# Expert weights of a mixture-of-experts stage in tiles of 256 whole rows instead of 512 half rows

## Chip, cores and metric

The kernel runs on one core of a Trainium2 chip. The metric is the device time of one execution, in microseconds (us); less is better.

## What is computed

The program is one mixing layer, a mixture-of-experts stage and two further layers on 512 tokens of 1024 channels. Only the middle stage is touched. Cut to what matters:

```
affinity = softmax(h @ w_router)                      # 512 tokens, 16 experts
gate_vals, tok_idx = top_k(affinity^T, 64)            # each expert takes 64 tokens
xs  = h[tok_idx]                                      # [16, 64, 1024]
hid = silu(xs @ w_gate[e]) * (xs @ w_up[e])           # per expert, 1024 x 1024 each
ye  = (hid @ w_down[e]) * gate_vals
out = zeros(512, 1024).at[tok_idx].add(ye)
```

The three weight matrices of an expert are 1024 x 1024 in float32, 4 MB each: 16 experts x 3 x 4 MB = 201 MB, each byte of which is read once.

## The kernel before

All names are of `_body`. Phase B (lines 1340 to 1673) is the experts' stage. It takes the 16 experts in eight pairs (`for p in range(8)`, L1585). A pair's 128 slots stand in the 128 partitions, 64 for each expert.

**The weights.** The list `wseq` (L1359 to L1364) says in which order tiles come. A tile is 1 MB: 512 rows of the matrix by half of its columns, [128, 4, 512] in SBUF, so each row of a tile is 2 KB contiguous in DRAM (`src`, L1379). A pair has 24 tiles, the program 192. `wload` (L1369) issues the next tile on SP's queue (L1381; the last two tiles in halves, L1387). The tiles rotate through `NW` = 11 buffers, and the 12th and 13th tile go into `macc`, which is still empty then. 13 tiles are issued ahead of the first use (L1391); afterwards `experts` calls `wload` twice each time it has used two tiles, and SP waits until the buffer's last reader has finished.

**The products.** `experts(p, W, n, lhs)` (L1539) fills one PSUM bank `pe` with 512 output columns (half `n`) for both experts, from four tiles: for each of 8 row blocks one matmul for each expert, in 64 of the array's columns each (L1551). One such matmul is recorded as two instructions.

**A pair, in the program's order.** For each half `n`: gate, then up (each four tiles), silu on ACT (L1618), the product with up on DVE (L1619), four transposes on PE (L1622) and a copy into `hidT` (L1623). In half 0 the slots' gates `gcol` and the transposed one-hot `ohT` are made besides (L1604 to L1616). Then `gather(p + 1)` (L1556) fetches the next pair's tokens by one-hot products (L1563, L1564) and transposes them into `xg` (L1570). Then, for each half of the output columns: down (four tiles), the scaled result split into `yh` on ACT (L1632) and `yl` on DVE (L1633), and the scatter: for four blocks of tokens two products with `ohT` (L1637, L1638), added into `macc` by DVE (L1643).

**PSUM.** Four banks with tag "g" for `pe`, four with tag "p" for all else (L1536). **The order.** A scheduler in the framework fixes the order on each engine when the program is built, which need not be the program's own; each engine then runs its list in sequence and waits only for data and buffers.

After the last pair the sums become the residual `xres` (L1651 to L1667), and phase C starts with the transposes at L1695.

```
            if i < len(wseq) - 2:
                nc.sync.dma_start(t, src)
...
                for e in range(2):
                    PE.matmul(o[64 * e:64 * e + 64], lhs(k, e), w[e][:, kk], start=k == 0, stop=k == 7)
            wload()
            wload()
```

Of the kernel before, what the change touches and what calls it, by code (L numbers as in the profile page):

```python
# [10 lines left out]
F32 = mybir.dt.float32  # L11
# [10 lines left out]
D = 1024  # L22
RH = 8
C = 64
# [103 lines left out]
def _body(tc, nc, st, A, out, dbg, stop):  # L128
# [13 lines left out]
    def rsqrt(pool, v, n, add, mul=1.0):  # L142
        """1/sqrt(v*mul+add) of a small tile v[:, :n], by Newton's steps."""
# [22 lines left out]
    # ---------------------------------------------------------------- phase A  # L166
# [52 lines left out]
    # silu(c) for the modulation: t = tanh(c/2); (t+1)*c = 2*silu(c)  # L219
# [30 lines left out]
    def mod_vec(j):  # L250
        """shift (j = 0, 1) or scale (2, 3) of 512 channels, by channel"""
# [11 lines left out]
    # normalised tokens, channel-major, split into two float32r parts  # L263
# [26 lines left out]
    def context():  # L290
        """what the first products need last: the context, and the other half of the channels"""
# [23 lines left out]
    def tok_major(c0, blocks, first=False):  # L315
        """blocks of h @ w_in[:, c0:c0+512], token-major, in PSUM"""
# [62 lines left out]
    def take():  # L379
        """the feed's next weights; the next but one are loaded and the next split before their products"""  # L380
# [7 lines left out]
    def ch_major(c0, ctxt, w=None):  # L388
        """(h @ w_in[:, c0:c0+128]).T in PSUM: the 512 tokens, and the context's 256"""
# [11 lines left out]
    # ------------------------------------------------------------ retention  # L401
# [7 lines left out]
    def late(t, name):  # L409
        """a table that is loaded no sooner than the modulation is there"""  # L410
# [15 lines left out]
    def rope_tok(dst, src, b, i):  # L426
        """rotary embedding of 8 heads, token-major (i = 1: times 1/8)"""
# [7 lines left out]
    def to_ch(dst, src, b):  # L435
        """dst[:, pair, b*128:...] = src.T for the four pairs of heads; dst: tiles and their partitions"""
# [8 lines left out]
    # each pair's heads, the other one's channels zero  # L445
# [83 lines left out]
    # gates, head norm: silu(g) * y * rsqrt(mean(y^2) + eps); t = tanh(g/2); (t+1)*g = 2*silu(g)  # L529
# [3 lines left out]
    def head_bcast(rs, pr, i, n):  # L533
        """rs: two parts of a row for each head of the pairs; every channel's of a pair"""
# [6 lines left out]
    # sums of squares over a head's 64 rows, in row 32*pair + 2*direction + head  # L541
# [37 lines left out]
    # ----------------------------------------------------------------- rwkv  # L579
# [5 lines left out]
    def wide(name, tag="W3", bufs=3):  # L585
        """one block of 128 channels: the 512 tokens, then the context's 256"""
# [20 lines left out]
    # 0 where a chunk begins, 1 elsewhere  # L607
# [23 lines left out]
    def mod_rest():  # L631
        """partial sums of the rest of the modulation's columns, for later; a step for every 256 rows"""
# [54 lines left out]
    # the retention's half of mix @ w_out  # L687
# [25 lines left out]
    # iclr = sigmoid(a0 + al @ a2) from th = tanh(z/2); kk = k*k_k / max(|k*k_k|, 1e-12)  # L713
# [13 lines left out]
    # sigmoid of the gates' inner columns  # L727
# [8 lines left out]
    # gt1*g_post_mix, g_pre_ffn*(1+sc2), sh2, gt2*g_post_ffn in rows 0, 32, 64, 96  # L736
# [34 lines left out]
    for pr in range(4):  # L771
# [28 lines left out]
        # cumulated decays of both directions, and what they multiply; direction 1 has a chunk's tokens reversed  # L800
# [24 lines left out]
        # the gates, and these times lnx_w  # L825
# [12 lines left out]
        # bonus + lnx_b, times the sum of the gates  # L838
# [66 lines left out]
    def batch(members, act):  # L905
        """four units (block of tokens, direction): products of their chunks' b, k with a, r"""
# [74 lines left out]
        # T21^T = T11^T A21^T T22^T  # L981
# [39 lines left out]
    def ready(u):  # L1021
        """what the chain needs of a unit: token-major b, k and v, decayed a and r above their products"""
# [26 lines left out]
    def decayed(u):  # L1049
        """a and r in place of b's products with them, which have been used"""  # L1050
# [8 lines left out]
    def step(u, c, ci, last):  # L1059
        """one chunk: u.UV[:, c] holds (state, v), then (u, v)"""  # L1060
# [55 lines left out]
    def spare(i):  # L1116
        """2 KB pieces of what held the context's products"""
# [6 lines left out]
    def finish(units):  # L1124
        """head norm of both units' outputs; gates and bonus, channel-major"""
# [54 lines left out]
    def chain(pair, last):  # L1180
        """two chunks of both directions, half a step apart"""
# [10 lines left out]
    class Weave:  # L1192
        """generators of work that is traced between others', at given rates"""
# [23 lines left out]
    def run(pairs, last=False):  # L1217
        """the chain over some pairs of units, directions alternating; the next pair is made ready meanwhile"""
# [63 lines left out]
    def load_out():  # L1282
        """the other half of w_out, in two parts; gt1*g_post_mix; g_pre_ffn*(1+sc2) and sh2 by channel"""
# [33 lines left out]
    # ---- mix @ w_out: the rwkv's half, in blocks of tokens as they end  # L1317
# [22 lines left out]
    # -------------------------------------------------- phase B: experts  # L1340
# [11 lines left out]
    # the mix and x; in their places the normed tokens' two parts  # L1352
# [16 lines left out]
    def wload():  # L1369
        i = wnext[0]  # L1370
        if i < len(wseq):
            W_, e, half, n = wseq[i]
            if NW <= i < NW + 2:
                # the sum of the experts is empty yet
                t = macc[:, 2 * (i - NW):2 * (i - NW) + 2].rearrange("p b (h n) -> p (b h) n", h=2)
# [27 lines left out]
    def rsqrt1(v):  # L1403
        """1/sqrt(v/D + EPS) of a column: the square root's reciprocal and one of Newton's steps"""
# [9 lines left out]
    # the router's weights times the gain, and its products with the shift  # L1414
# [9 lines left out]
    def mixed(tb):  # L1424
        """x + gt1 * rms_norm(mix)"""
# [873 lines left out]
```

## Time and profile before

| | us |
|---|---|
| median of 3 runs (2916.70 to 2926.42) | 2918.49 |
| span of the profiled execution | 2929.8 |
| own time of the profiled execution | not given beside its span |
| experts' products, first to last | 818.6 to 1316.9 |
| PE busy over the span | 2724.7 (93%) |

The profile is of one execution; times in it count from the span's start. PE is the matmul engine, PEld its weight load, DVE, ACT, POOL the vector, scalar and general engines, SP the engine that issues most DMAs. A view by stretches gives each engine's busy time in that stretch, the granted PE clock as a share of full speed, the mean busy share of the 16 DMA engines (it can read over 1, since a packet's time runs from read to write) and the rate at which they moved bytes.

### The profile page before, as it was taken

To read this page: it belongs to the slowest core of one execution; us is meant where nothing else is said; L and a number is where in the kernel's file an instruction comes from. 1 tells how busy PE (TensorE), PEld (TensorE's weight loads), DVE (VectorE), ACT (ScalarE), POOL (GpSimd) and SP (SyncE) were. 2 spreads that over 40 slices of the span, in tenths; PEclk is the share of its full clock that TensorE was granted. 3 is DMA by queue.
4 is the path that set the end of the run, shared out by engine and by line. 5 is a ranking of instruction groups with operands and counts; after the bars stand their busy time and mean duration, and the time that the engine had idled before them with its cause. 6 is when DMAs were issued, how large, how long until landed. Compare 5 with 4: busy or idle time off the path is not lost.

```text
span 2929.8 us, 38119 instructions
## 1 busy us (share of the span) xinstructions
PE 2724.7 (93%) x15198; PEld 1930.5 (66%) x15198; DVE 1358.2 (46%) x2452; ACT 1026.0 (35%) x1988; POOL 266.3 (9%) x266
## 2 busy tenths in 40 slices
PE   7999997578899888888999999989999999999999
PEld 5767555457743333336778767867888888888887
DVE  4354286897611111116545655456334444444333
ACT  4232353356421101115445534643223332333223
POOL 1102044545100000002000000000000000000000
PEclk9999977789899999998999989988999999999999
DMA  6305755546779999993212311232222333223332
GB/s 244 87 15 175 233 163 160 140 113 167 265 291 386 386 387 387 387 373 116 58 58 72 102 51 51 65 117 64 94 94 94 94 91 96 88 93 94 94 94 93
DMA packets 300433, 456.33 MB, mean 156 GB/s; under 512 B 32367, under 2 KB 127160, under 8 KB 299744
## 3 DMA queue, kind: packets, MB, share of 16 engines
q1 hardware_dynamic: 283376, 438.44, 45.0%
q10 hardware_dynamic: 13632, 7.79, 0.9%
q0 software_dynamic: 3248, 7.67, 0.8%
q8 instruction: 120, 1.97, 0.3%
q14 instruction: 57, 0.47, 0.0%
HBM read 425.45 MB, written 28.40 MB: 155 GB/s over the span
## 4 chain that ended last, share of the span: by engine, by line
PE 67%; DMA 7%; DVE 6%; ACT 1%; issue 1%; POOL 0%; SPq 0%; DVEq 0%; ACTq 0%; POOLq 0%
PE acc L1771 10%; PE acc L1773 10%; PE acc L1772 10%; PE pe L1551 8%; PE accb L162 6%; PE accb L163 6%; PE accb L164 6%; DMA wexp<-in_w_up 3%; DMA wexp<-in_w_gate 2%; PE pS L2053 2%; DVE zT L971 1%; DVE zZ L973 1%; PE po L2105 1%; PE pt L1936 1%; DMA xres<-sx 1%
## 5 line engine op out<-in xcount | busy, mean ns | idle before, releaser
L159 DVE TENSOR_TENSOR wlo<-wc,whi 128x1024 fp32r<-128x1024 f32 x238 | 291.2, 1224 | 483.3 <-ACT whi L158 468.8
L158 ACT CAST whi<-wc 128x1024 fp32r<-128x1024 f32 x240 | 251.8, 1049 | 499.6 <-PE acc L1772 313.9
L1771 PE MATMUL acc<-whi,yHi 128*128 128x512 f32 x640 | 274.1, 430 | 5.0 <-DVE xres L1805 4.6
L163 PE MATMUL accb<-y2Lo,whi 128*128 128x512 f32 x704 | 278.4, 395 | 0.0
L162 PE MATMUL accb<-y2Hi,whi 128*128 128x512 f32 x704 | 277.6, 396 | 0.1
L164 PE MATMUL accb<-y2Hi,wlo 128*128 128x512 f32 x704 | 277.5, 395 | 0.0
L1551 PE MATMUL pe<-wexp,xg 128*64 128x512 f32 x1008 | 245.0, 597 | 30.7 <-DMA wexp<-in_w_up 21.3
L1773 PE MATMUL acc<-wlo,yHi 128*128 128x512 f32 x640 | 257.5, 403 | 0.0
L1772 PE MATMUL acc<-whi,yLo 128*128 128x512 f32 x640 | 256.5, 401 | 0.0
L1771 PE MATMUL acc<-whi,aHi 128*128 128x512 f32 x512 | 202.7, 396 | 0.0
L1772 PE MATMUL acc<-whi,aLo 128*128 128x512 f32 x512 | 202.6, 396 | 0.0
L1773 PE MATMUL acc<-wlo,aHi 128*128 128x512 f32 x512 | 202.5, 396 | 0.0
L1551 PEld LDWEIGHTS pe<-wexp,xg 128*64 128x64 f32 x1008 | 77.0, 136 | 174.8 <-issue 122.5
L1771 PEld LDWEIGHTS acc<-whi,yHi 128*128 128x128 f32 x640 | 130.9, 205 | 42.4 <-issue 15.4
L162 PEld LDWEIGHTS accb<-y2Hi,whi 128*128 128x128 f32 x704 | 131.9, 187 | 32.7 <-ACT whi L158 0.5
L163 PEld LDWEIGHTS accb<-y2Lo,whi 128*128 128x128 f32 x704 | 132.0, 187 | 32.4 <-DVE y2Lo L1698 0.3
L164 PEld LDWEIGHTS accb<-y2Hi,wlo 128*128 128x128 f32 x704 | 132.0, 187 | 32.1
L1773 PEld LDWEIGHTS acc<-wlo,yHi 128*128 128x128 f32 x640 | 130.6, 204 | 28.5 <-issue 4.6
L1772 PEld LDWEIGHTS acc<-whi,yLo 128*128 128x128 f32 x640 | 131.5, 205 | 20.4 <-issue 1.4
L1551 PE MATMUL pe<-wexp,hidT 128*64 128x512 f32 x512 | 123.8, 597 | 1.9 <-DMA wexp<-in_w_down 1.9
L1771 PEld LDWEIGHTS acc<-whi,aHi 128*128 128x128 f32 x512 | 96.2, 188 | 23.2
L1773 PEld LDWEIGHTS acc<-wlo,aHi 128*128 128x128 f32 x512 | 96.2, 188 | 23.2
(654 smaller groups left out, 4617.9 us busy)
## 6 DMA issues: line engine op xcount, KB each, us to landing
wc<-in_mlp_w SPq DMA_DIRECT2D x128, 512.0 KB
wexp<-in_w_gate SPq DMA_DIRECT2D x63, 1024.0 KB
wexp<-in_w_up SPq DMA_DIRECT2D x63, 1024.0 KB
wexp<-in_w_down SPq DMA_DIRECT2D x62, 1024.0 KB
wc<-in_a_wqkv SPq DMA_DIRECT2D x72, 512.0 KB
wmod<-in_w_mod SPq DMA_DIRECT2D x32, 512.0 KB
w_b<-in_w_in SPq DMA_DIRECT2D x24, 512.0 KB
wc<-in_b_win SPq DMA_DIRECT2D x24, 512.0 KB
```

Source lines behind the costliest of these rows:

```text
L158: ACT.copy(hi, src)
L159: eng.tensor_tensor(lo, src, hi.bitcast(F32), op=OP.subtract)
L162: PE.matmul(o, whi, xhi, start=first, stop=False)
L163: PE.matmul(o, whi, xlo, start=False, stop=False)
L164: PE.matmul(o, wlo, xhi, start=False, stop=last)
L971: V.tensor_tensor(tm, Z[:, j + 1:, j:j + 1].to_broadcast([128, m, j]), Z[:, j:j + 1, :j].to_broadcast([128, m, j]), op=OP.mult)
L973: V.tensor_tensor(Z[:, j + 1:, :j], Z[:, j + 1:, :j], tm, op=OP.add)
L1551: PE.matmul(o[64 * e:64 * e + 64], lhs(k, e), w[e][:, kk], start=k == 0, stop=k == 7)
L1771: PE.matmul(acc[b], xh, hi[:, kk], start=k == 2 * halves[0], stop=False)
L1772: PE.matmul(acc[b], xl, hi[:, kk], start=False, stop=False)
L1773: PE.matmul(acc[b], xh, lo[:, kk], start=False, stop=k == 2 * halves[-1] + 1)
L2053: PE.matmul(pS[:, x * wd + lo:x * wd + hi], qT[r, pr, b * 128:(b + 1) * 128], kT[r, pr, ks], start=True, stop=True)
```

## The change

Each tile holds 256 whole rows of a matrix, [128, 2, 1024], 4 KB contiguous in DRAM, still 1 MB. `expert_quarter` uses two such tiles (one for each expert) for both halves of the output columns, so gate, up and down each accumulate in two PSUM banks at once. Silu for both halves follows gate, the product with up for both halves follows up. `gather` and `scatter` become generators: the scatter's split into `yh` and `yl` follows down, its products are kept in `owed` and run after the first two quarters of the next pair's gate. The last pair's down keeps the old tiles and order (`expert_half`, which is the old `experts`, and an immediate scatter). Buffers, their number and the number of loads stay. Lines that only lose a comment are left out here; they shift line numbers.

```diff
-        for n, W_ in ((0, "w_gate"), (0, "w_up"), (1, "w_gate"), (1, "w_up"), (0, "w_down"), (1, "w_down")):
-            for half in range(2):
-                for e in range(2):
-                    wseq.append((W_, 2 * p_ + e, half, n))
+        for W_ in ("w_gate", "w_up"):
+            wseq += [(W_, 2 * p_ + e, i, None) for i in range(4) for e in range(2)]
+        if p_ < 7:
+            wseq += [("w_down", 2 * p_ + e, i, None) for i in range(4) for e in range(2)]
+        else:
+            wseq += [("w_down", 2 * p_ + e, half, n) for n in range(2) for half in range(2) for e in range(2)]
...
-                t = pool.tile([128, 4, 512], F32, tag=tag, name="wexp")
-            src = A[W_][0, e, half * 512:half * 512 + 512, n * 512:n * 512 + 512].rearrange("(k p) n -> p k n", p=128)
+                t = pool.tile([128, 2, D] if n is None else [128, 4, 512], F32, tag=tag, name="wexp")
+            if n is None:
+                src = A[W_][0, e, part * 256:part * 256 + 256].rearrange("(k p) n -> p k n", p=128)
+            else:
+                src = A[W_][0, e, part * 512:part * 512 + 512, n * 512:n * 512 + 512].rearrange("(k p) n -> p k n", p=128)
...
+    def expert_quarter(p, W, i, o, lhs):
...
+        for kk in range(2):
+            k = 2 * i + kk
+            for n in range(2):
+                for e in range(2):
+                    PE.matmul(o[n][64 * e:64 * e + 64], lhs(k, e), w[e][:, kk, n * 512:n * 512 + 512], start=k == 0, stop=k == 7)
+        wload()
+        wload()
...
+        g = [ps("pe", "g") for _ in range(2)]
+        for i in range(4):
+            expert_quarter(p, "w_gate", i, g, xl)
+            if owed and i < 2:
+                next(owed.pop(0))
+        sgs = []
         for n in range(2):
-            g = experts(p, "w_gate", n, xl)
-            u = experts(p, "w_up", n, xl)
...
+            sgs.append(E2.tile([128, 512], F32, name="sg_"))
+            ACT.activation(sgs[n], g[n], AF.Silu)
+        u = [ps("pe", "g") for _ in range(2)]
+        for i in range(4):
+            expert_quarter(p, "w_up", i, u, xl)
...
+        for n in range(2):
+            V.tensor_tensor(sgs[n], u[n], sgs[n], op=OP.mult)
         if p < 7:
-            xg = gather(p + 1)
+            nxt = gather(p + 1)
+            next(nxt)
...
+        if p < 7:
+            y = [ps("pe", "g") for _ in range(2)]
+            for i in range(4):
+                expert_quarter(p, "w_down", i, y, hl)
+            for n in range(2):
+                s_ = scatter(p, n, y[n], gcol, ohT)
+                next(s_)
+                owed.append(s_)
```

What this moves on the engines, at three places. First, SP's queue from the last loads of the phase before to the second pair (`xb` is a block of x, `wexp` a weight tile, `macc` the sum's place used as a tile). Before:

```order
L1358 DMA xb<-in_x 128x1024
L1381 DMA wexp<-in_w_gate 128x4x512 x4
L1381 DMA wexp<-in_w_up 128x4x512 x4
L1381 DMA wexp<-in_w_gate 128x4x512 x3
L1381 DMA macc<-in_w_gate 128x4x512
L1381 DMA macc<-in_w_up 128x4x512
L1381 DMA wexp<-in_w_up 128x4x512 x3
L1381 DMA wexp<-in_w_down 128x4x512 x8
```

Now:

```order
L1358 DMA xb<-in_x 128x1024
L1386 DMA wexp<-in_w_gate 128x2x1024 x8
L1386 DMA wexp<-in_w_up 128x2x1024 x3
L1386 DMA macc<-in_w_up 128x2x1024 x2
L1386 DMA wexp<-in_w_up 128x2x1024 x3
L1386 DMA wexp<-in_w_down 128x2x1024 x8
```

The number of loads is the same; their shape is not, and a matrix's eight tiles follow each other.

Second, PE from a pair's down into the next pair's gate, in the steady pairs (`hidT` is the hidden layer, `xg` the tokens, `psc` the scatter's products). Before:

```order
L1551 MATMUL pe<-wexp,hidT 64x512 x14
L1637 MATMUL psc<-yh,ohT 128x512 x2
L1638 MATMUL psc<-yl,ohT 128x512 x2
L1637 MATMUL psc<-yh,ohT 128x512
L1638 MATMUL psc<-yl,ohT 128x512
L1637 MATMUL psc<-yh,ohT 128x512
L1638 MATMUL psc<-yl,ohT 128x512
L1551 MATMUL pe<-wexp,hidT 64x512 x15
L1551 MATMUL pe<-wexp,xg 64x512
L1637 MATMUL psc<-yh,ohT 128x512 x2
```

Now:

```order
L1555 MATMUL pe<-wexp,hidT 64x512 x32
L1617 MATMUL psc<-yh,ohT 128x512 x4
L1618 MATMUL psc<-yl,ohT 128x512 x2
L1555 MATMUL pe<-wexp,xg 64x512 x2
L1618 MATMUL psc<-yl,ohT 128x512 x2
L1617 MATMUL psc<-yh,ohT 128x512
L1618 MATMUL psc<-yl,ohT 128x512
L1617 MATMUL psc<-yh,ohT 128x512
L1618 MATMUL psc<-yl,ohT 128x512
L1617 MATMUL psc<-yh,ohT 128x512
L1555 MATMUL pe<-wexp,xg 64x512 x6
L1618 MATMUL psc<-yl,ohT 128x512
```

Down runs through, and both halves of the scatter stand among the first eight products of the next gate.

Third, PE at the end of up in the steady pairs (`sg_` is the gated product, `pgat` the gather). Before:

```order
L1551 MATMUL pe<-wexp,xg 64x512 x25
L1622 MATMUL pt<-k_ident,sg__7454 128x128 x4
L1551 MATMUL pe<-wexp,xg 64x512 x31
L1551 MATMUL pe<-wexp,hidT 64x512
L1622 MATMUL pt<-k_ident,sg__7513 128x128 x4
L1563 MATMUL pgat<-hi,oh 128x512
L1564 MATMUL pgat<-lo,oh 128x512
```

Now:

```order
L1583 MATMUL pgat<-hi,oh 128x512
L1584 MATMUL pgat<-lo,oh 128x512
L1555 MATMUL pe<-wexp,xg 64x512 x46
L1682 MATMUL pt<-k_ident,sg__7436 128x128 x4
L1682 MATMUL pt<-k_ident,sg__7438 128x128 x4
L1591 MATMUL pgat<-k_ident,xt 128x128 x8
L1555 MATMUL pe<-wexp,hidT 64x512 x32
```

The gather's products have moved ahead, among gate and up; all transposes of a pair stand together between up and down. In phase C each engine's order is the same as before.

## Rows read from the trace of the kernel before

**Rows 1.** The page: span, DMA busy share and rate in 40 slices.

```profile
span 2929.8 us, 38119 instructions
DMA  6305755546779999993212311232222333223332
GB/s 244 87 15 175 233 163 160 140 113 167 265 291 386 386 387 387 387 373 116 58 58 72 102 51 51 65 117 64 94 94 94 94 91 96 88 93 94 94 94 93
```

**Rows 2.** Busy time by stretches; last columns PE clock, DMA share, GB/s.

```profile
840.00:860.00 20.00, 19.15 (x94) 8.62 (x92) 2.33 (x5) 4.10 (x8) 0.00 (x0) 1.00 1.05 387
...
1250.00:1300.00 50.00, 42.88 (x201) 15.47 (x198) 4.78 (x8) 3.84 (x7) 0.00 (x0) 1.00 1.05 387
```

**Rows 3.** PE alone by stretches: one pair each (the second, fifth, sixth).

```profile
875.30:933.00 57.70, 54.25 (x262) 1.00 1.05 386
1059.90:1126.30 66.40, 57.13 (x263) 1.00 1.05 387
1126.30:1191.50 65.20, 57.02 (x262) 1.00 1.05 386
```

**Rows 4.** PE's waits, second pair (876 to 933 us): total, times, longest.

```profile
PE psc L1637 <- ACT yh L1632: 1.7, 2, 0.8
PE pt L1622 <- DVE sg__7187 L1619: 0.8, 1, 0.8
```

**Rows 5.** PE's waits in the fifth pair (1060 to 1126 us), the two longest.

```profile
PE pe L1551 <- DMA wexp<-in_w_up: 4.3, 3, 1.6
PE pe L1551 <- DMA wexp<-in_w_gate: 1.9, 2, 1.6
```

**Rows 6.** DMA queues in 900 to 1260, 2004 to 2005, 23 to 25, 762 to 764 us.

```profile
DMA packets 69852, 139.16 MB, mean 387 GB/s; under 512 B 2125, under 2 KB 2125, under 8 KB 69837
...
DMA packets 341, 0.35 MB, mean 349 GB/s; under 512 B 0, under 2 KB 341, under 8 KB 341
...
DMA packets 244, 0.81 MB, mean 405 GB/s; under 512 B 27, under 2 KB 27, under 8 KB 244
...
DMA packets 216, 0.79 MB, mean 395 GB/s; under 512 B 23, under 2 KB 23, under 8 KB 216
```

**Rows 7.** SP's issues behind those stretches: start, us, line, tensor.

```profile
18.05 0.82 SPq L207 DMA_DIRECT2D xin<-in_ctx  x2
...
760.48 0.43 SPq L1358 DMA_DIRECT2D xb<-in_x  x1
...
2002.30 0.37 SPq L1746 DMA_DIRECT2D wc<-in_mlp_w  x1
```

**Rows 8.** The weight stream's start: PE, SP, then two stretches, one later.

```profile
818.61 13.95 PE L1551 MATMUL pe<-wexp,xg 128*64 128x512 f32 x64
...
822.29 3.80 SPq L1381 DMA_DIRECT2D wexp<-in_w_up  x3
...
823.00:824.00 1.00, 1.00 (x8) 0.39 (x6) 0.00 (x0) 0.00 (x0) 0.00 (x0) 1.00 0.61 43
824.00:825.00 1.00, 1.00 (x6) 0.29 (x4) 0.00 (x0) 0.00 (x0) 0.00 (x0) 1.00 0.83 309
825.00:826.00 1.00, 1.00 (x8) 0.33 (x6) 0.00 (x0) 0.18 (x1) 0.00 (x0) 1.00 1.06 412
```

**Rows 9.** The first pair's down begins, in order of time.

```profile
854.81 1.08 PE L1551 MATMUL pe<-wexp,hidT 128*64 128x512 f32 x4
```

**Rows 10.** The last pair and the scatter's adds, in order of time.

```profile
1256.94 2.48 DVE L1643 TENSOR_TENSOR macc<-psc,macc 128x512 f32<-128x512 f32 x4 [0.59 <-PE psc L1638]
...
1292.16 3.22 PE L1551 MATMUL pe<-wexp,xg 128*64 128x512 f32 x13 [1.64 <-DMA wexp<-in_w_up]
...
1303.00 3.82 PE L1551 MATMUL pe<-wexp,hidT 128*64 128x512 f32 x16 [1.58 <-DMA wexp<-in_w_down]
...
1309.86 7.08 PE L1551 MATMUL pe<-wexp,hidT 128*64 128x512 f32 x30
```

**Rows 11.** The chain that ended last: phase C's first transposes.

```profile
1336.28 1.11 PE pt L1695 x4
```

More of the change, by code (lines that the diff above doesn't have):

```diff
@@ L1537, in _body, with expert_half @@
     E2 = pb_.enter_context(tc.tile_pool(name="E2", bufs=2))
-    def experts(p, W, n, lhs):
+    def expert_quarter(p, W, i, o, lhs):
+        w = []
+        for e in range(2):
+            key, t = wtiles.pop(0)
+            assert key == (W, 2 * p + e, i, None)
+            w.append(t)
+        for kk in range(2):
+            k = 2 * i + kk
+            for n in range(2):
+                for e in range(2):
+                    PE.matmul(o[n][64 * e:64 * e + 64], lhs(k, e), w[e][:, kk, n * 512:n * 512 + 512], start=k == 0, stop=k == 7)
+        wload()
+        wload()
+    def expert_half(p, W, n, lhs):
         o = ps("pe", "g")
@@ L1583, in _body, with scatter @@
     V.memset(epsb, EPS)
-    xg = gather(0)
+    _, xg = gather(0)
+    def scatter(p, n, y, gcol, ohT, moe=None):
+        yh = E2.tile([128, 512], F32R, name="yh")
+        yl = E2.tile([128, 512], F32R, name="yl")
+        ACT.activation(yh, y, AF.Copy, scale=gcol)
+        V.scalar_tensor_tensor(yl, y, gcol, yh.bitcast(F32), op0=OP.mult, op1=OP.subtract)
+        yield
+        for b in range(4):
+            o = ps("psc")
+            l = ohT[:, b * 128:(b + 1) * 128]
+            PE.matmul(o, l, yh, start=True, stop=False)
+            PE.matmul(o, l, yl, start=False, stop=True)
+            m = macc[:, b, n * 512:(n + 1) * 512]
+            if p == 0:
+                ACT.copy(m, o)
+            else:
+                V.tensor_tensor(m, o, m, op=OP.add)
+            if moe:
+                t = E2.tile([128, 512], F32, name="sg_")
+                ACT.activation(t, m, AF.Square, accum_out=ss3[:, n, b:b + 1])
+                V.tensor_tensor(moe[b][:, n * 512:(n + 1) * 512], m, bc3[:, n * 512:(n + 1) * 512], op=OP.mult)
+        yield
+    owed = []
     for p in range(8):
@@ L1616, in _body @@
                 ACT.copy(ohT, pt)
-            sg_ = E2.tile([128, 512], F32, name="sg_")
-            ACT.activation(sg_, g, AF.Silu)
-            V.tensor_tensor(sg_, u, sg_, op=OP.mult)
-            pt = ps("pt")
-            for i in range(4):
-                PE.transpose(pt[:, i * 128:(i + 1) * 128], sg_[:, i * 128:(i + 1) * 128], ident)
-            ACT.copy(hidT[:, 4 * n:4 * n + 4].rearrange("p i s -> p (i s)"), pt)
+        for n in range(2):
+            V.tensor_tensor(sgs[n], u[n], sgs[n], op=OP.mult)
         if p < 7:
-            xg = gather(p + 1)
+            nxt = gather(p + 1)
+            next(nxt)
         else:
@@ L1628, in _body @@
         for n in range(2):
-            y = experts(p, "w_down", n, lambda k, e: hidT[:, k, 64 * e:64 * e + 64])
-            yh = E2.tile([128, 512], F32R, name="yh")
-            yl = E2.tile([128, 512], F32R, name="yl")
-            ACT.activation(yh, y, AF.Copy, scale=gcol)
-            V.scalar_tensor_tensor(yl, y, gcol, yh.bitcast(F32), op0=OP.mult, op1=OP.subtract)
-            for b in range(4):
-                o = ps("psc")
-                l = ohT[:, b * 128:(b + 1) * 128]
-                PE.matmul(o, l, yh, start=True, stop=False)
-                PE.matmul(o, l, yl, start=False, stop=True)
-                m = macc[:, b, n * 512:(n + 1) * 512]
-                if p == 0:
-                    ACT.copy(m, o)
-                else:
-                    V.tensor_tensor(m, o, m, op=OP.add)
-                if p == 7:
-                    t = E2.tile([128, 512], F32, name="sg_")
-                    ACT.activation(t, m, AF.Square, accum_out=ss3[:, n, b:b + 1])
-                    V.tensor_tensor(moe[b][:, n * 512:(n + 1) * 512], m, bc3[:, n * 512:(n + 1) * 512], op=OP.mult)
-            if p == 7 and n == 0:
-                ACT.activation(warm2, ss3[:, 0, 3:4], AF.Sqrt)
+            pt = ps("pt")
+            for i in range(4):
+                PE.transpose(pt[:, i * 128:(i + 1) * 128], sgs[n][:, i * 128:(i + 1) * 128], ident)
+            ACT.copy(hidT[:, 4 * n:4 * n + 4].rearrange("p i s -> p (i s)"), pt)
+        if p < 7:
+            xg = next(nxt)
+        hl = lambda k, e: hidT[:, k, 64 * e:64 * e + 64]
+        if p < 7:
+            y = [ps("pe", "g") for _ in range(2)]
+            for i in range(4):
+                expert_quarter(p, "w_down", i, y, hl)
[3 more added lines that the diff above has]
+                owed.append(s_)
+        else:
+            for n in range(2):
+                for _ in scatter(p, n, expert_half(p, "w_down", n, hl), gcol, ohT, moe):
+                    pass
+                if n == 0:
+                    ACT.activation(warm2, ss3[:, 0, 3:4], AF.Sqrt)
     s3, rstd, w3, a3 = (E2.tile([128, 4], F32, name=n, bufs=1) for n in ("s3", "rstd", "w3", "a3"))
```

9 lines of the change are left out of this document (5 added, 4 removed).

## The prediction

> **What bounds the kernel now.** I read the page's slices first. In slices 13 to 17 of 40, some 370 us, the DMA row stands at 9 and the rate at 386 or 387 GB/s; nowhere else does it stay there [rows 1]. That is the experts' stage. Then the view by stretches: 387 GB/s at a DMA share of 1.05 near its start and at its end alike, PE's clock at 1.00, which is the upper of its two levels, 2.4 GHz [rows 2]. So the stage might be bound by the weight stream. PE is also busy there, so I took it pair by pair. The second pair takes 57.7 us and waits for no weights, because the 13 tiles loaded ahead are not used up yet; the sixth takes 65.2 us [rows 3]. The waits say why: in the second pair PE stands only for the scatter's split (1.7 us) and the gated product (0.8 us, twice; one is shown) [rows 4]; in the fifth the longest are for weights [rows 5]. A wait is short because it is counted between products that each need a new tile.
>
> The stream accounts for the length. A tile has 1.0486 MB; at 387 GB/s [rows 6] that is 2.710 us, and a pair's 24 tiles take 65.0 us, against 65.2 measured. The stream restarts at about 824, when PE has used the first two tiles (PE starts at 818.61, SP issues at 822.29, the data run from 824) [rows 8]. From there to the last wait for a tile at 1303.00, the second half of the last pair's first down [rows 10], are 479 us; the tiles in it are 192 - 13 - 4 = 175, by 2.710 = 474 us. The other 5 us are the ramp and small transfers. **The stage is the DMA stream from end to end**; behind it comes a chain on PE, ACT and DVE from 1303 to phase C's transposes at 1336.28 [rows 11], which the change leaves as it is.
>
> **What a tile costs after the change.** A tile has the same bytes in 256 runs of 4 KB instead of 512 of 2 KB. No long stream of 4 KB runs is in this trace, so I take it from run lengths. Rates of loads without gaps [rows 6]: 349 GB/s at 1 KB (from 2004, a load of an MLP's weights; 341 packets for 0.35 MB), 387 at 2 KB. For 16 engines that is 16 x 1024 / 349 = 46.9 ns and 16 x 2048 / 387 = 84.7 ns a packet: 37.7 ns for each KB and about 9 ns for each packet whatever its size. A 4 KB packet by this line: 84.7 + 2 x 37.7 = 160.1 ns, 409 GB/s, 2.564 us a tile. The short stretches with mostly 4 KB runs (ctx tokens at 23, x and the mix at 762 [rows 7], some tiny packets among them) moved 405 and 395 GB/s [rows 6]. They are two microseconds long, and a fresh 2 KB stream also reads 412 in one such microsecond [rows 8], so they neither prove nor refute it.
>
> Bounds: 395 GB/s gives 2.655 us a tile (0.055 saved); 412, the most that any of these rows shows, gives 2.545 (0.165). I take 409, since the line joins the two lengths with nothing else among them; its weakness is that the 1 KB load is 1 us of the trace.
>
> The Trainium skill, in "DMA: Bandwidth & Descriptors", section SWDGE vs HWDGE vs iDMA, lists 408.7 GB/s for a core's load stream of 1 MiB DMAs with 4 KiB rows issued from SP; by it a tile would take 2.566 us, an estimate, and the sum below would be 24.6 us instead of 25.0.
>
> **The sum.** Of the 179 tiles after the 13 early ones the last 8 keep their 2 KB rows, so 171 change: 171 x (2.710 - 2.564) = 25.0 us less. All of it lies on the path, as long as PE keeps below the stream.
>
> *PE as cover.* A pair would take 24 x 2.564 = 61.5 us on the stream. PE needs 57.7 us without waiting for weights [rows 3], of which the change removes some: one of two waits for `yh` (0.8) and parts of the two for the gated product [rows 4], since the gather's products or the other half's transposes now stand there. It adds switches between weight products and others, where the scatter and the gather are woven into gate and up: some eight a pair. I allow 0 to 0.4 us each, less than one `yh` wait. PE stays at 55 to 60 us: price nothing, cover 1.5 to 6 us a pair.
>
> *The first pairs.* While the first pair's up ends and its gather runs, no buffer comes free. 16 tiles are used by then, two of them in `macc`, so 14 loads are out: 14 x 2.564 = 35.9 us from 824, until 859.9. Before, down began at 854.81 [rows 9]; its first two tiles are used 3.5 us later (16 records at the 13.95 us for 64 of [rows 8]), at 858.3, and new data follow 1.7 us behind the issue (822.29 to 824): 860.0. So the stream just holds; 0 to 2 us, I take 0.
>
> *SP and the other engines.* As many loads as before, in one queue, each behind the release of its buffer; half the runs to write out. The 13 early tiles end sooner and nobody waits for them before 818.61: nothing. Silu, the gated product and the adds are the same number of instructions at other times; a gate's second bank is free when down needs it, because silu follows gate. Nothing, covered by the stream.
>
> *The end.* Behind the last up tile four 2 KB tiles must land before the last wait: 1292.16 to 1303.00, 10.8 us [rows 10]. In it PE now has both halves' transposes, one half more than before, and waits for the tiles all the same. Nothing. The last down has the old order.
>
> The profiled span, 2929.8 us, becomes 2904.8. It is 0.4% over the median of the runs shown, 2918.49, and the execution's own time is not given beside it; I take the same 25.0 us off the median: **2893.5 us**.
>
> **Rivals.**
>
> 1. *Run length does not matter in a stream.* 387 GB/s would then be a limit on bytes. For it: the DMA share stands at 1.05 in all stretches [rows 2], and the 4 KB rows above are short. Against it: the 1 KB load at 349. Time: 2918.5. It would come to the same if the 4 KB runs were cut to 2 KB on the way. 10%. The Trainium skill has a rule for it (same page, Specifications: transfers of 512 B or more run at line rate); by that rule nothing is gained here. The trace speaks against it: 1 KB and 2 KB loads differ by 11% [rows 6].
>
> 2. *PE becomes the bound.* If the woven order costs more than I allow, a pair takes PE's time once the early tiles are used up, some five pairs. At 64 us instead of 61.5: 5 x 2.5 = 12.5 us given back, 2906. For it: the cover is only 3.8 us by [rows 3]. Against it: the removed waits. 8%.
>
> 3. *Slower: the scatter stalls PE.* Eight scatter groups now follow each other through the four "p" banks, each emptied by an add on DVE, and the one-hot's transposes and the gather take the same banks. PE runs in order, so a full set of banks holds the weight products behind it, these hold the buffers, and SP cannot load. It decides when a pair on PE passes 65.0 us, 7.3 us more than now; at 67 us, over seven pairs, it costs 14 us: 2932. For it: the two halves were four tiles of down apart and are now together. Against it: four adds take 2.48 us [rows 10], eight 5 us, and PE's own sixteen products lie beside them, so what is left is some 1 to 2 us. 4%.
>
> **How the numbers follow.** My forecast has 78%. By the bounds it lies between 171 x 0.165 = 28 us and 171 x 0.055 = 9.4 us less: 2890 to 2909; with 2 us of the first pair's gap and the runs' own scatter 2886 to 2910, which holds the second rival also: 80% or a little more. A measurement of this kernel tells some 0.3%, 8.8 us, from no change. Faster by more: 78 + 8 = 86%; within: 10%; slower: 4%.
>
> **What would show it.** In the profile after: 405 to 412 GB/s from 826 to about 1275, then 387 for the last eight tiles; steady pairs of 61 to 62 us; PE still waiting for weights from the fourth pair on; the last wait for down near 1278 and phase C's transposes near 1311, with the same 33 us between them. If the rate rises and the pairs don't shorten by as much, PE's waits will name `psc`, `pt` or `pgat` instead of weights (rivals 2 and 3). If the rate stays at 387, the first rival holds. A rate below 395 or a gain above 30 us would prove the line over run lengths wrong.

## The result, and the profile after

The changed kernel takes 2899.75 us (median of 4 runs, 2895.5 to 2906.07), the kernel before beside it 2922.45 (4 runs): ratio 0.9919, 95% interval 0.9892 to 0.9946, so 16 to 32 us less. The forecast was 2893.5 in 2886 to 2910. A later set of runs gave the changed kernel 2897.34 against 2917.99, ratio 0.9913 (0.9879 to 0.9946). Between the profiled executions the span fell from 2929.8 to 2904.2, by 25.6 us; the sum said 25.0.

The page of the changed kernel, the rows that answer to [rows 1]:

```profile
span 2904.2 us, 38123 instructions
...
DMA  6205755436779999983122211232222223222222
GB/s 246 81 22 170 232 176 164 145 105 168 268 283 409 408 409 409 409 307 121 51 63 91 70 59 59 66 109 66 94 94 94 94 89 94 94 93 95 93 93 92
```

The plateau stands at 409 where it stood at 387, and its last slice falls from 373 to 307, three quarters of the plateau. Outside slices 13 to 18 the row is much as it was.

The stage has clear ends, the first and the last weight product. The groups of products that write `pe`, kernel before; the columns are count, shortest, median and longest ns, first and last start in us:

```profile
L1551 PE MATMUL pe<-wexp,xg x1008: 592/592/644, 818.6 to 1295.2; 128*64 128x512 f32 x168
L1551 PE MATMUL pe<-wexp,hidT x512: 592/592/644, 848.3 to 1316.3; 128*64 128x512 f32 x171
```

The same of the changed kernel:

```profile
L1555 PE MATMUL pe<-wexp,xg x1008: 592/592/643, 815.9 to 1267.0; 128*64 128x512 f32 x168
...
L1571 PE MATMUL pe<-wexp,hidT x64: 592/592/644, 1269.0 to 1288.1; 128*64 128x512 f32 x64
```

From 818.6 to 1316.3 are 497.7 us, from 815.9 to 1288.1 472.2: **25.5 us less, the whole difference of the spans**. What lies outside the stage is 2432.1 and 2432.0 us. (That these two are so equal is chance: over the runs below whose program is the same there, span less stage goes from 2422 to 2428, and where a table is built ahead of the stage from 2433 to 2445. So I compare stages, and leave what is under some 10 us in a total open.)

The DMA queues from 900 to 1200 us, before:

```profile
DMA packets 58195, 115.99 MB, mean 387 GB/s; under 512 B 1771, under 2 KB 1771, under 8 KB 58182
```

and after:

```profile
DMA packets 31774, 122.59 MB, mean 409 GB/s; under 512 B 1879, under 2 KB 1879, under 8 KB 31761
```

A little over half the packets, and 5.7% more bytes in the same 300 us. The view by stretches of the changed kernel, for [rows 2] (the last columns are PE's clock, DMA share and GB/s):

```profile
1000.00:1050.00 50.00, 49.80 (x215) 21.32 (x215) 8.14 (x14) 6.49 (x12) 0.00 (x0) 1.00 1.03 409
...
1250.00:1270.00 20.00, 18.26 (x72) 6.52 (x69) 1.38 (x2) 1.17 (x2) 0.00 (x0) 1.00 1.03 400
1270.00:1280.00 10.00, 8.07 (x35) 2.87 (x31) 0.73 (x1) 0.69 (x1) 0.00 (x0) 1.00 1.05 386
```

The last eight tiles, which kept their 2 KB runs, move at 386 again. But the first row also has something that I did not expect: PE is busy for 49.80 of 50 us, in the middle of a stage that the stream was to bind. PE's waits over the whole stage (818 to 1320 us; total, times, longest) name weights only here:

```profile
PE pe L1555 <- DMA wexp<-in_w_up: 1.5, 3, 0.6
...
PE pe L1571 <- DMA wexp<-in_w_down: 1.3, 1, 1.3
...
PE pe L1555 <- DMA wexp<-in_w_down: 0.5, 1, 0.5
```

All of these fall in the last pairs. Counted from one pair's `pgate` products (they make the gates `gcol`) to the next's, the third to seventh pairs took 61.9, 65.0, 66.3, 65.2 and 67.1 us before, and 59.9, 59.8, 60.3, 61.4 and 63.0 after: below the 61.5 of the stream as long as the lead of tiles lasts. The pairs that grow longer show where their wait has gone. The weight products (`pe`) of the third and of the sixth pair; the first number behind the length is PE's busy time:

```profile
932.00:991.90 59.90, 47.90 (x192) 17.17 (x192) 2.88 (x4) 2.57 (x4) 1.00 1.03 407
...
1112.00:1173.40 61.40, 49.47 (x192) 17.43 (x192) 2.89 (x4) 2.57 (x4) 1.00 1.03 409
```

The products are the same and so is their order, yet they take 47.90 us in the third and fourth pairs, 48.27 in the fifth, 49.47 in the sixth and 50.05 in the seventh. So a busy PE proves no bound here: in the later pairs part of the wait for weights counts as busy time, and the list of waits, which counts idle time alone, leaves it out. So two things could set the 472 us, the stream or PE's own 59.9 us a pair, 1.6 us apart. The experiments had to tell these apart, and the run length from the other two parts of the change.

### The profile page after: what moved, and what is told of

It reads as the page before. It is cut to its first block, busy times and chain, and to the rows that moved or that the text cites. A ratio compares the mean times of both kernels' runs of the same rounds, so it can differ in the third digit from the quotient of the medians.

```text
span 2904.2 us, 38123 instructions
## 1 busy us (share of the span) xinstructions
PE 2746.8 (95%) x15198; PEld 1951.0 (67%) x15198; DVE 1360.5 (47%) x2452; ACT 1024.9 (35%) x1988; POOL 268.2 (9%) x266
## 4 chain that ended last, share of the span: by engine, by line
PE 72%; DVE 6%; DMA 3%; ACT 1%; issue 0%; POOL 0%; SPq 0%; DVEq 0%; ACTq 0%
PE pe L1555 11%; PE acc L1822 10%; PE acc L1824 10%; PE acc L1823 10%; PE accb L162 6%; PE accb L163 6%; PE accb L164 6%; PE pS L2104 2%; DVE zZ L973 2%; DVE zT L971 2%; DMA wexp<-in_w_down 1%; PE po L2156 1%; PE pt L1987 1%; PE pf L2233 1%; DMA xres<-sx 1%; PE pgat L1583 1%
## 5 line engine op out<-in xcount | busy, mean ns | idle before, releaser
L1555 PE MATMUL pe<-wexp,xg 128*64 128x512 f32 x1008 | 263.7, 597 | 1.5 <-DMA wexp<-in_w_up 1.5
L1555 PEld LDWEIGHTS pe<-wexp,xg 128*64 128x64 f32 x1008 | 89.2, 136 | 150.9 <-issue 144.9
L1823 PEld LDWEIGHTS acc<-whi,aLo 128*128 128x128 f32 x512 | 96.2, 188 | 23.3
```

The lines of the kernel that those rows point to most:

```text
L1555: PE.matmul(o[n][64 * e:64 * e + 64], lhs(k, e), w[e][:, kk, n * 512:n * 512 + 512], start=k == 0, stop=k == 7)
L1823: PE.matmul(acc[b], xl, hi[:, kk], start=False, stop=False)
```

## The experiments

All with the profile; the ratio is to the kernel before on the same chip.

| kernel | runs | GB/s, 900 to 1200 | pairs 3 to 7, us | stage, us | ratio (95% interval) |
|---|---|---|---|---|---|
| before | 2 KB | 387 | 61.9, 65.0, 66.3, 65.2, 67.1 | 497.7 | 1 |
| changed | 4 KB | 409 | 59.9, 59.8, 60.3, 61.4, 63.0 | 472.2 | 0.9919 (0.9892 to 0.9946) |
| changed order, 2 KB runs | 2 KB | 387 | 64.5, 65.0, 66.6, 65.0, 66.3 | 497.6 | 1.0003 (0.9983 to 1.0022) |
| scatter at once | 4 KB | 409 | 59.6, 59.6, 60.9, 61.4, 63.0 | 472.2 | 0.9917 (0.9899 to 0.9936) |
| before, 1 KB runs | 1 KB | 348 | 71.3, 72.6, 72.8, 73.6, 73.1 | 550.2 | 1.0174 (1.0145 to 1.0203) |
| both experts in a tile | 4 KB | 409 | 56.9, 61.4, 62.9, 61.4, 62.7 | 471.4 | 0.9923 (0.9899 to 0.9946) |
| 8 KB runs | 8 KB | 416 | 59.8, 59.9, 59.9, 59.9, 62.2 | 464.4 | 0.9894 (0.9872 to 0.9917) |
| 8 KB runs, operand reordered | 8 KB | 414 | 60.1, 60.0, 60.1, 60.0, 62.1 | 464.5 | 0.9948 (0.9931 to 0.9964) |
| 8 KB runs, both experts in a tile | 8 KB | 420 | 60.0, 59.8, 60.2, 60.9, 61.1 | 469.2 | 0.9964 (0.9947 to 0.9982) |
| 8 KB runs, table by a load | 8 KB | 414 | 60.0, 60.0, 60.0, 60.0, 62.4 | 464.6 | 0.991 (0.9881 to 0.994) |
| changed, again | 4 KB | 409 | 59.8, 59.8, 60.3, 61.6, 62.8 | 472.2 | 0.9913 (0.9879 to 0.9946) |

**The order and the scatter without the run length.**

```diff
-                src = A[W_][0, e, part * 256:part * 256 + 256].rearrange("(k p) n -> p k n", p=128)
+                r, c = part // 2 * 512, part % 2 * 512
+                t = t.rearrange("p k (h n) -> p (k h) n", h=2)
+                src = A[W_][0, e, r:r + 512, c:c + 512].rearrange("(k p) n -> p k n", p=128)
```

> The changed kernel with the same 1 MB tiles, the same number of loads and the same order on every engine, but each tile fetched as 512 half rows of 2 KB instead of 256 whole rows of 4 KB (the weights so stand in other places of the tile, so another product is computed). Theory A (the run length sets the stream's rate, and the stream the time): 387 GB/s again, steady pairs of 65 us, span about 2929, ratio to before 0.998 to 1.003; PE waits for weights some 5 us a pair. Rival B (the new order of the products and the later scatter made the gain): rate above 400 or not, the span stays near 2904, ratio 0.990 to 0.993. Rival C (each gave a part): between, near 2917.

The queues, 900 to 1200 us:

```profile
DMA packets 58184, 115.95 MB, mean 387 GB/s; under 512 B 1776, under 2 KB 1776, under 8 KB 58171
```

The stage is 497.6 us, as before the change, and the ratio 1.0003. With the changed order, the both-halves products and the deferred scatter, but 2 KB runs, nothing is gained: **the gain needs the run length, and the other parts give nothing without it.** Two expectations were missed. The span, 2920.0 for about 2929, differs outside the stage. And PE's waits for weights are 6.8 us from 940 to 1200 us, 1.7 a pair and not 5; the rest stands in the products, which take 51.54 us in the fourth pair where the same order took 47.90 with 4 KB runs:

```profile
992.00:1057.00 65.00, 51.54 (x192) 17.48 (x192) 2.88 (x4) 2.57 (x4) 1.00 1.05 387
```

**The run length without the scatter's move.**

```diff
-            if owed and i < 2:
-                next(owed.pop(0))
...
-                next(s_)
-                owed.append(s_)
+                for _ in s_:
+                    pass
```

> Edit: the changed kernel without its second part: the scatter's products of a pair stand in the program directly behind its down products again, not in the next pair's gate. Theory 1 (the time comes from the run length alone; where the scatter's products stand hardly matters, since the scheduler puts them among the next gate's products either way and TensorE is not the bound): stage 470 to 474 us as in the changed kernel (472.2), ratio to the kernel before 0.990 to 0.995. Theory 2 (the deferral carries part of the gain: TensorE, which has only 1.5 us a pair to spare, stalls at the scatter's wait for the scaled outputs): 1 to 3 us more in each of seven pairs, stage 479 us or more, ratio 0.996 or more.

Stage 472.2, to the tenth that of the changed kernel. The deferral is worth nothing here: the scheduler puts the scatter among the next gate's products (`xg`) in either case. PE in order of time (start, us, line, form, records) without the deferral:

```profile
983.21 1.07 PE L1618 MATMUL psc<-yl,ohT 128*128 128x512 f32 x4
984.21 1.07 PE L1555 MATMUL pe<-wexp,xg 128*64 128x512 f32 x2
985.22 0.50 PE L1617 MATMUL psc<-yh,ohT 128*128 128x512 f32 x1
```

**The other direction: the kernel before with 1 KB runs.**

```diff
             if i < len(wseq) - 2:
-                nc.sync.dma_start(t, src)
+                for h in range(2):
+                    nc.sync.dma_start(t[:, :, h * 256:h * 256 + 256], src[:, :, h * 256:h * 256 + 256])
```

> The kernel before, each tile (but the last two) fetched by two loads of half its columns, 1 KB runs. The line over run lengths: 349 GB/s, 3.00 us a tile instead of 2.71, 177 tiles after the early ones: 52 us more, span about 2982, ratio to before 1.016 to 1.020. If run length did not matter: ratio 1.000. If the doubled number of loads cost more than the runs: over 1.022.

The queues, 900 to 1200 us:

```profile
DMA packets 105016, 104.45 MB, mean 348 GB/s; under 512 B 3178, under 2 KB 105004, under 8 KB 105004
```

348 GB/s over 300 us, against the 349 of a single microsecond in [rows 6], and a stage 52.5 us longer. The weak end of the line over run lengths holds.

**Stream or PE: the same bytes and run length, the two experts' rows in one tile.** The place to look is how PE issues the products. In the changed kernel an expert's tile carries 256 rows of one expert, and the scheduler issues some products of one expert ahead of the other's. PE in order of time, changed kernel (start, us, line, form, records):

```profile
968.13 14.01 PE L1555 MATMUL pe<-wexp,hidT 128*64 128x512 f32 x64
...
983.70 1.93 PE L1555 MATMUL pe<-wexp,xg 128*64 128x512 f32 x4
985.56 0.74 PE L1618 MATMUL psc<-yl,ohT 128*128 128x512 f32 x2
```

64 records of alternating experts take 14.01 us, 0.22 each: each fills one half of the array's columns (128*64), and two run together. Four records between the scatter's, of one expert alone, take 1.93. A tile of 128 rows of both experts lets them be neighbours again:

```diff
-                src = A[W_][0, e, part * 256:part * 256 + 256].rearrange("(k p) n -> p k n", p=128)
+                src = A[W_][0, e:e + 2, part * 128:part * 128 + 128].rearrange("e p n -> p e n")
...
-                    PE.matmul(o[n][64 * e:64 * e + 64], lhs(k, e), w[e][:, kk, n * 512:n * 512 + 512], start=k == 0, stop=k == 7)
+                    PE.matmul(o[n][64 * e:64 * e + 64], lhs(k, e), t[:, e, n * 512:n * 512 + 512], start=k == 0, stop=k == 7)
```

> The changed kernel with a tile that holds one block of 128 rows of both experts (1 MB, 4 KB runs as before), so that both experts' products become ready together and stay next to each other in PE's order. Theory A: the stream is the bound at 409 GB/s, so the span stays at 2904 (2901 to 2905), ratio 0.991 to 0.993, while PE's pairs without waits fall from 59.9 towards 56 us and its waits for weights come back, 4 to 6 us a pair. Rival E (PE has become the bound, its single products cost the time): the span falls by 5 us or more and PE's waits for weights stay under 2 us a pair.

The same view of that kernel:

```profile
983.36 1.94 PE L1552 MATMUL pe<-wexp,xg 128*64 128x512 f32 x8
```

Eight records in the time of four. The weight products of one pair (24 tiles, 192 records), first number behind the length; the kernel before:

```profile
994.90:1059.90 65.00, 44.84 (x192) 14.07 (x192) 2.88 (x4) 2.57 (x4) 1.00 1.05 386
```

the changed kernel:

```profile
991.90:1051.70 59.80, 47.90 (x192) 17.19 (x192) 2.89 (x4) 2.57 (x4) 1.00 1.03 409
```

both experts in a tile:

```profile
982.00:1042.00 60.00, 43.97 (x192) 12.42 (x192) 2.88 (x4) 2.57 (x4) 1.00 1.03 409
```

So 3.9 us of PE's pair go. And the waits for weights are back (940 to 1180 us, both experts in a tile):

```profile
PE pe L1552 <- DMA wexp<-in_w_down: 10.9, 18, 0.7
PE pe L1552 <- DMA wexp<-in_w_up: 6.5, 11, 0.6
```

The third pair falls to 56.9 us, the later ones come back to 61 to 63, and the stage is 471.4 against 472.2: what PE gained it waits. **In the changed kernel the stage's length is the stream's**; PE's slower products cost nothing, by a margin of 1.6 us a pair. The span, 2895.1, missed the 2901 to 2905, and by its 9 us alone would speak for rival E. But 8.3 of them lie outside the stage, where the two programs are the same; the waits and the ratio, 0.9923, are theory A's.

**The next run length, 8 KB.**

```diff
-                src = A[W_][0, e, part * 256:part * 256 + 256].rearrange("(k p) n -> p k n", p=128)
+                src = A[W_][0, e, part * 256:part * 256 + 256].rearrange("(p k) n -> p k n", p=128)
```

> The changed kernel with each tile fetched as 128 runs of 8 KB (two neighbouring rows to a partition, without putting the other operand in that order, so another product is computed); the order on every engine is the same. Theory A with the line over run lengths (9 ns a packet and 37.7 ns a KB): 311 ns a packet, 421 GB/s if nothing else binds, 59.7 us a pair. PE's own pace in the changed kernel was 59.9 us a pair, so stream and PE would be level: a pair of 59.9 to 60.2, span 2893 to 2896, ratio to before 0.987 to 0.990. Rival D (no gain beyond 4 KB, a limit on bytes near 409 GB/s): span 2904, ratio 0.992.

The queues, 900 to 1200 us:

```profile
DMA packets 17180, 124.67 MB, mean 416 GB/s; under 512 B 1908, under 2 KB 1908, under 8 KB 2036
```

The third to sixth pairs take 59.8 to 59.9 us, without a wait for weights in them and with 47.90 us of weight products in each: PE keeps its own pace. The stage gets 7.8 us shorter, where a stream that still bound would have given 171 tiles by 2.564 less 2.497 (1.0486 MB at the 420 GB/s that the page's full slices reach), 11.5 us. The same 300 us in 40 slices, GB/s, and SP's loads of up in the third pair:

```profile
GB/s 422 419 419 422 397 285 412 425 421 416 421 421 416 418 419 419 417 418 423 423 418 417 422 422 417 424 418 421 416 414 422 419 416 423 418 422 416 425 419 421
...
914.73 28.94 SPq L1386 DMA_DIRECT2D wexp<-in_w_up  x8
```

The stream has one hole, at 930 to 945 us: SP's eight loads are spread to 943.67, each behind the release of a buffer by PE. An estimate from these slices puts the loss at some 3 us, most of the 3.7 that are missing. Behind it 24 tiles at 420 GB/s take 59.9 us, PE's own time. PE is the bound of the middle pairs now, but the stream is level with it, as expected. That is the edge of the second rival, met one step later.

**The 8 KB runs with the reference's product.** The other operand has to have its rows in the same order: its transposes read every second column, and the norm's gains stand in a second table.

```diff
+        xv = xt.rearrange("p (i q t) -> p i t q", i=4, t=2)
...
-                PE.transpose(pt[:, k * 128:(k + 1) * 128], xt[:, (k0 + k) * 128:(k0 + k + 1) * 128], ident)
+                PE.transpose(pt[:, k * 128:(k + 1) * 128], xv[:, (k0 + k) // 2, k % 2], ident)
...
+                for t in range(2):
+                    PE.transpose(pv[:, 16 + 8 * t:24 + 8 * t], g8v[:, t], ident[:8, :8])
...
+                ACT.copy(gsp, pv[:, 16:32])
```

> Edit: the changed kernel with runs of 8 KB, as in the run with 8 KB, but with the other operand put in the same order of rows (two transposes of each pair read every second column; a second table of the norm's gains is built once), so that the reference's product is computed. Theory 1 (the stream brings a pair in about 60 us, and TensorE's products as woven now take 59.9): pairs of 59.8 to 60.5 us, no wait for weights from the second to the sixth pair, the experts' stage from first to last weight product 463 to 467 us (472.2 in the changed kernel), ratio to the kernel before 0.987 to 0.991. Theory 2 (reading every second column of fp32 slows TensorE's transposes or their copies, and these stand on TensorE's path now that it sets the pace): pairs of 60.5 to 62 us and a stage of 468 us or more, ratio 0.991 to 0.994.

The stage is 464.5 us, as the first theory had it, but the ratio only 0.9948. Its ends (first and last weight product):

```profile
L1562 PE MATMUL pe<-wexp,xg x1008: 592/592/643, 826.2 to 1270.0; 128*64 128x512 f32 x168
...
L1578 PE MATMUL pe<-wexp,hidT x64: 592/592/643, 1272.0 to 1290.7; 128*64 128x512 f32 x64
```

It begins at 826.2, 10 us later than in the changed kernel's profile (815.9). PE in order of time ahead of it:

```profile
777.90 1.94 PE L1458 MATMUL pt<-k_ident,xres 128*128 128x128 f32 x8 [5.19 <-issue]
779.77 3.20 PE L1462 MATMUL pl<-wrg,h2T 128*64 128x16 f32 x32
782.90 1.97 PE L1458 MATMUL pt<-k_ident,xres 128*128 128x128 f32 x8
```

In the changed kernel these transposes started at 771.71 and were woven with the router's products (12, 8, 3, 24 records, and so on); here they stand block by block behind a hole of 5.2 us. The edit ahead of the stage is two small transposes and a copy, 60 us earlier; the run after next tests whether they led the scheduler to this order.

**PE's pace by itself: 8 KB runs and both experts in one tile of 2 MB.**

```diff
+            wseq += [(W_, 2 * p_, i, None) for i in range(4)]
...
+                t = pool.tile([128, 2, 2, D] if n is None else [128, 2, 4, 512], F32, tag=tag, name="wexp")
...
+                src = A[W_][0, e:e + 2, part * 256:part * 256 + 256].rearrange("e (p k) n -> p e k n", p=128)
```

> Edit: as the corrected kernel with 8 KB runs, but one tile holds 256 rows of both experts of a pair (2 MB, one load), in 4 places and macc's, so that the two experts' products become ready together and are issued as neighbours. Theory 1 (TensorE's 59.9 us a pair come from the two experts' products having been put apart, each running alone in half of the array; put together again, TensorE needs some 55 us a pair and the stream with 8 KB runs is the bound again): products of the two experts overlap all through, TensorE waits for weights again, and the pairs fall to the stream's own time, 24 tiles of 1.0486 MB at 416 to 421 GB/s, 59.8 to 60.5 us, so nothing is gained over the kernel with 8 KB runs: stage 461 to 467 us. Theory 2 (TensorE was holding back the stream in the 8 KB run, whose real rate is higher): rate above 421 GB/s, pairs of 56 to 59 us, stage under 460 us. Theory 3 (the coarser places, 10 MB of tiles in 5 instead of 13 MB in 13, starve the stream): holes in the DMA slices, under 410 GB/s, stage 470 us or more.

The queues, 900 to 1200 us:

```profile
DMA packets 16401, 125.97 MB, mean 420 GB/s; under 512 B 970, under 2 KB 970, under 8 KB 1098
```

A pair's weight products:

```profile
1001.80:1061.60 59.80, 43.19 (x192) 13.18 (x192) 2.88 (x4) 2.57 (x4) 1.00 1.01 420
```

PE's waits, 940 to 1180 us:

```profile
PE pe L1560 <- DMA wexp<-in_w_down: 12.4, 12, 1.4
PE pe L1560 <- DMA wexp<-in_w_up: 6.8, 8, 1.3
```

43.19 us of weight products a pair for 47.90, and 19.2 us of waits in four pairs, 4.8 each: PE needs 55.2 us, the stream 60. So PE's pace, 4.7 us a pair faster, shortens no pair: the stream alone gives 60 us. The first theory holds for the third to fifth pairs (60.9 and 61.1 behind them are over its 60.5). Its stage of 461 to 467 us was missed, 469.2: with five large places only 10 tiles are loaded ahead for 13, and three tiles more at 2.49 us are 7.5 us. That reading is worked out, not tried by itself.

**8 KB runs with the order ahead of the stage kept.**

```diff
-                for t in range(2):
-                    PE.transpose(pv[:, 16 + 8 * t:24 + 8 * t], g8v[:, t], ident[:8, :8])
...
+        nc.gpsimd.dma_start(gsp.rearrange("p (c t) -> p c t", t=2), sBC[1:3].rearrange("r (i p t) -> p (r i) t", p=128, t=2))
```

> Edit: the corrected kernel with 8 KB runs, but the second table of gains comes by one strided load on POOL's queue in place of two transposes and a copy. In the corrected kernel the experts' stage was 464.5 us, but began at 826.2 us (815.9 in the changed kernel), because the two transposes and the copy led the scheduler to another order before it: transposes of the second norm's input and router products block by block (8, 32, 8, 32) instead of woven, after a 5 us hole. Theory 1 (that order is the whole delay): with the order of the changed kernel back, the stage begins at 811 to 819 us and takes 463 to 466 us; ratio to the kernel before 0.987 to 0.991, some 0.3% under the changed kernel. Theory 2 (the delay is due to something else, such as a slower clock before the stage): it still begins after 822 us, ratio 0.993 to 0.996. The strided load has 1024 packets of 8 bytes: some us on its queue long before it is wanted, nothing on the path.

And the changed kernel once more beside it:

> Edit: none; the changed kernel again, beside the one above on the same chip, so that the two are compared within one set of runs. Expected: ratio to the kernel before 0.990 to 0.994, stage from first to last weight product 472 us plus or minus 1.

The ends of the stage with 8 KB runs:

```profile
L1557 PE MATMUL pe<-wexp,xg x1008: 592/592/644, 821.2 to 1265.2; 128*64 128x512 f32 x168
...
L1573 PE MATMUL pe<-wexp,hidT x64: 592/592/643, 1267.2 to 1285.8; 128*64 128x512 f32 x64
```

464.6 us, against 472.2 (818.1 to 1290.3) in the changed kernel beside it. The woven order is back, and the start 5 us earlier than in the kernel with the two transposes, yet 2 us outside the 811 to 819 that I had written down. The last product of the mix (`acc`), which stands ahead of the reordered ones, tells what is the order's; changed kernel, with the two transposes, and with the load:

```profile
769.78 0.39 PE L1328 MATMUL acc<-Wo,mix 128*128 128x512 f32 x1
...
770.62 0.40 PE L1335 MATMUL acc<-Wo,mix 128*128 128x512 f32 x1
...
774.99 0.39 PE L1330 MATMUL acc<-Wo,mix 128*128 128x512 f32 x1
```

From there to the first weight product (815.9, 826.2, 821.2) are 46.1, 55.6 and 46.2 us. So the order cost 9.4 us, and the load brings all of it back; the 5.2 us that are left are there at the mix's last product already, in a part that the order doesn't touch. The totals are 2896.99 and 2897.34 us, ratios 0.991 and 0.9913: the 7.6 us of the stage don't show in the time. In these two profiles they lie in the later start (3.1 us) and behind the stage (1610.8 for 1605.7 us from its last product's end), in parts that the two programs share, and span less stage varies by as much over the other runs. I don't call it a better kernel.

## Why the prediction was right, and where it was not

- **The bound** (the stage is the weight stream from end to end): right. The run that made PE faster left the stage at 471.4; the one with 2 KB runs had the old stage.
- **The price of a tile** (160.1 ns a packet, 409 GB/s, 2.564 us): measured 409. The line over run lengths, 37.7 ns for each KB and 9 for each packet, was drawn through 1 and 2 KB; it gives 421.6 GB/s at 8 KB (310.9 ns), and the run in which the stream bound at 8 KB moved 420. The Trainium skill's 408.7 GB/s ("DMA: Bandwidth & Descriptors", section SWDGE vs HWDGE vs iDMA) agrees with 409; its rule that 512 B are enough for line rate (same page, Specifications) does not: 348, 387, 409 and 420 GB/s at 1, 2, 4 and 8 KB.
- **The sum** (171 tiles, 25.0 us): 25.5 in the stage, 25.6 in the spans. The median came out at 2899.75 for 2893.5; 4 us of that are the kernel before, 2922.45 in that set and not 2918.49, and the two medians lie 22.7 us apart. That the spans came so near to 25.0 is luck, since what lies outside the stage varies by more than the miss.
- **The first pairs and the end** (nothing): the stream holds through the first pair's gap, which lies ahead of the slices at 409, with PE busy all through:

```profile
845.00:865.00 20.00, 20.00 (x102) 9.62 (x102) 2.80 (x6) 4.77 (x10) 0.00 (x0) 1.00 1.03 409
```

  The chain of waits of the changed kernel, in order of time:

```profile
1260.52 14.25 DMA wexp<-in_w_down
1274.81 3.66 PE pe L1571 x15
...
1308.07 1.12 PE pt L1746 x4
```

  The last wait for down ended at 1274.81 and the transposes began at 1308.07 (1278 and 1311 foreseen). Between them are 33.3 us, as before (1303.00 to 1336.28, [rows 10, 11]); 2.7 of the 3 us are the stage's earlier start.
- **PE as cover** was the step that failed in its detail. "PE still waiting for weights from the fourth pair on" was not seen as idle time, which is listed in the last pairs alone, 3.3 us; by the longer products the wait sets in with the fifth pair (0.4 us) and reaches 1.6 and 2.2 in the sixth and seventh. I had priced the weaving as "some eight switches a pair", 0 to 0.4 us each, 3.2 at most. The rows show something else: the weaving, with tiles of one expert each, splits pairs of products that run together, and a product alone takes the time of two. The weight products of the second pair, which the working rested on, kernel before:

```profile
875.30:933.00 57.70, 42.52 (x192) 13.26 (x192) 2.88 (x4) 2.57 (x4) 1.00 1.05 386
```

  They take 42.52 us there and 47.90 in the third pair of the changed kernel, 5.4 more, where both kernels have no wait for weights. (The 44.84 before, shown above, are of a pair that waits.) That is nearly the whole growth of PE's busy time, from 54.25 us [rows 3] to 59.7; against it the waits of 3.3 us in the second pair [rows 4, with the one not shown] fell to 0.2, more than I had taken off. So PE's pair is 59.9 us, the top of "55 to 60", by two errors that partly cancel. The cover was there, 1.6 us a pair of the 1.5 to 6 I allowed, so the time came out, but narrowly; with 1.6 us more of it a pair PE would have been the bound, the second rival. At 8%, with the cover at its lowest bound, it was given too little.
- **The third rival** (scatter stalls PE): from 940 to 1180 us the list has no wait of PE but 0.2 us now and then for the gated product, none for `psc`. **The first** fell by the rate.
- What the change calls its other parts (order, both halves at once, deferred scatter) gave nothing by themselves in the run with 2 KB runs, and the deferral nothing with 4 KB either. Both halves at once came with the whole rows, which bring both halves; whole rows without them were not tried.

## What to carry to other kernels

Where a stage moves bytes at a flat rate with the DMA share over 1, count packets: fit time per packet over the run lengths that the trace already has, and price longer rows by it; stop when the time per tile falls under the compute engine's own. Before trusting that engine's cover, look at what the new tiles let the scheduler pull apart: two products in opposite halves of the array are cheap only as neighbours. Don't take a busy engine for the bound: compare its busy time for the same work in a stretch that doesn't wait. And when a variant's stage is shorter but its total isn't, compare where the stage starts, since a small edit far ahead can reorder what leads up to it.

## What was not expected of the hardware

A product in 64 of the 128 columns takes as long alone as two in opposite halves together: 4 records in 1.93 us, 8 in 1.94. The Trainium skill ("TensorEngine Tiling (Array Packing)", Tiling Modes, Key Properties) says that different tiles of the array can run products in parallel; the trace agrees, and adds that in these kernels it happened where the two stood next to each other in the engine's order. A wait for weights can also stand in a profile as busy time: the same 192 records in the same order took 47.90 us where tiles came early, and 49.47 (4 KB runs, sixth pair) and 51.54 (2 KB runs, fourth pair) where they came late. That lone products cause it, one expert's tile being there and the other's not, is my reading, not shown by a run of its own. And one core's loads went on to 420 GB/s with 8 KB runs, with no sign of a limit on bytes up to there.
